# A hybrid decoder layer in split fp32: the sums of the MLP's input, its stores, kept factors of w1 and the late loads change places

## The chip, the cores and the metric

The kernel runs on one core of one Trainium2 chip. A core has five engines with queues of their own: TensorE (PE in the profile; its weight loads are PEld), VectorE (DVE), ScalarE (ACT), GpSimd (POOL) and SyncE (SP), which here only issues DMAs. An engine works through its queue in order. The metric is the device time of one execution in microseconds (us).

## The reference

One decoder layer over 2048 tokens of width 1024, all in fp32:

```python
h = rms_norm(x, mix_norm_pre)
z = h @ w_in                                  # q, k, v, xr, gr
attn = dilated_attention(q, k, v)             # 8 heads, 3 dilations, one joint softmax of the branches
rec  = rg_lru(causal_conv(xr)) * gelu(gr)     # linear recurrence
x = x + rms_norm(concat([attn, rec]) @ w_out, mix_norm_post)
h = rms_norm(x, mlp_norm_pre)
a = relu(h @ w_ff_in)                         # 1024 x 4096
x = x + rms_norm((a * a) @ w_ff_out, mlp_norm_post)
```

## The kernel before

**Products.** A matrix product in fp32 is made of three matmuls in the type fp32r: each operand is split into a high part, a cast by ScalarE, and a low part, operand minus high part (`split`, L52 to L55: the cast is L54, the subtraction L55). The products are high by high, high by low and low by high. Who subtracts is an argument: VectorE as a rule, GpSimd where `lo_eng` says so.

**Stages.** The tokens are worked in two halves of 1024 (`hf` 0 and 1). First come the input projections and the recurrence of both halves, with the attention of half 0. Then, for half 0: the out-projection (`OutProj`; matmuls L778 to L780), the MLP's input (`mlp_in`; L934 to L936) and the MLP's output (`mlp_out`; L1064 to L1066). The attention of half 1 is woven into the MLP's output of half 0 by `interleave`: so many matmul steps of the MLP (`fill`) after each piece of attention. Then come the out-projection and the MLP of half 1. From the out-projection of half 0 on, TensorE's order is the order of the program text. The other engines' order is made by a scheduler that simulates the program; `tc.issue_after(i)` forbids it to issue something ahead of instruction `i`.

**The MLP's input.** `mlp_in` multiplies by a scheme with seven products in place of eight for 2x2 blocks. The right operands B11, B21, B22 and T1 to T4 are sums of blocks of the normed tokens; `Factors.columns` makes B11, B21 and T3 column block by column block while the out-projection runs, `Factors.late` T2, T4, T1 and B22 after it. The left operands come from w1: 16 pairs `j`, each with two loads of 512 KB (`w1r`; for the first two pairs the first of them is `w1f`), four sums on GpSimd (`sub`, L945: S1, S3 in the place of a21, S2, S4 in the place of a12; S1 and S2 are the tiles `ws1` and `ws2`) and seven splits into the tiles `f<half>_<pair>_<product>H` and `L`. A product is 12 matmuls. The program works on two pairs at a time (`TURNS`). ScalarE copies sums out of PSUM (L969 is that of z22 and one of three), VectorE adds, ScalarE squares; `sq` and `as` are what comes out, and SP stores them to DRAM as `sa` (L995, 0.75 MB and L996, 1 MB a pair). `sq`, `as` and `w2s`, the sums of the w2 blocks made on VectorE in half 0 and stored by GpSimd's queue as `sb` (L1007), share a ring of four buffers with one another ("ring r"). A second ring holds six pairs of f tiles, and a third one the w1 tiles.

**The MLP's output.** For each of seven products and 16 `j`, SP loads an `a` and a `b` factor (L1056) from `sa` and from `sb` or `sw2`, and they are split in place (`a_5L` is the low part of a's factor of j 5). At the end of half 1, tokens 12 to 15 get their norm, gain and residual ahead of the last product (`finish`: GpSimd multiplies by the gain, L1097; VectorE adds the residual `x2e`, L1100, loaded at L1095), and tokens 8 to 11 afterwards (`finish_left`, its load is L1109; `finish_right`).

**The join.** At the end of each pair of heads, `join` works out the weights of the branches, stores them (`sco`, L638), loads them back spread over the partitions (`co`, L645), and GpSimd sums the two branches (L647 to L649) and stores them into `smix` (L650). `mix_columns` loads columns of `smix` (L752, 64 KB each, four to a tile `m_0L` or `m_4L`) for the out-projection.

Of the kernel before, what the change touches and what calls it, by code (L numbers as in the profile page):

```python
# [51 lines left out]
def split(nc, hi, lo, src, lo_eng=None):  # L52

    nc.scalar.copy(out=hi, in_=src)  # L54
    return (lo_eng or nc.vector).tensor_tensor(out=lo, in0=src, in1=f32(hi), op=ALU.subtract)  # L55
# [31 lines left out]
class Project:  # L87


    def __init__(self, tc, p, pa, pl, bank, cst, scr, x, xT, g1, w_in):  # L90
# [112 lines left out]
    def qkv(self, hf, pr):  # L203
# [148 lines left out]
def attention(tc, p, bank, cst, scr, hf, mask_a_d, mask_b_d, pj, pw=None, px=None):  # L352
# [255 lines left out]
    def join(pr, st, na, nb):  # L608

        R = 2 * NQH  # L610
        pst = bank("o", f"pst{hf}_{pr}")
# [25 lines left out]
        for i, e in enumerate((eA, eB)):  # L637
            nc.sync.dma_start(out=scr["co"][hf][pr][i].rearrange("h (n j) -> (h n) j", j=P), in_=e)  # L638
        for b in range(NBH):
# [3 lines left out]
            for i in range(2):  # L643
                for u in range(2):
                    nc.sync.dma_start(out=co[i][u * HD:(u + 1) * HD, :],  # L645
                                      in_=scr["co"][hf][pr][i, u:u + 1, cs].partition_broadcast(HD))
# [98 lines left out]
def mix_columns(nc, sh, scr, hf, order, t):  # L745

    mx = {}
    for g0 in range(0, KT, 4):
        n = f"{hf}_{t}_{g0}"
        hi, lo = sh.pair(f"m{n}", (P, 4, P))  # L750
        for i, k in enumerate(order[g0:g0 + 4]):
            nc.sync.dma_start(out=f32(lo[:, i, :]), in_=scr["mix"][hf][k][:, t * P:(t + 1) * P])  # L752
# [154 lines left out]
def mlp_in(tc, sh, scr, hf, H, w1, w2, first):  # L907
# [8 lines left out]
    def pair(j):  # L916
# [4 lines left out]
        def load(f):  # L921
            t = first[j] if f == 0 and j < len(first) else sh.w(f"w1r{n}_{f}", (P, KT, P))
# [22 lines left out]
        sub = lambda o, x, y, op=ALU.subtract: g.tensor_tensor(out=o, in0=x, in1=y, op=op)  # L945
# [10 lines left out]
        S1, S2 = [sh.s(f"ws{i}_{n}", (P, KH, P)) for i in (1, 2)]  # L956
        sub(S1, a21, a22, ALU.add)
        sub(a21, a11, a21)
        factor(7, a21)
        sub(S2, S1, a11)  # L960
        sub(a12, a12, S2)
# [33 lines left out]
        nc.sync.dma_start(out=scr["a"][hf][j][:, 0:3], in_=sq[:, 0:3])  # L995
        nc.sync.dma_start(out=scr["a"][hf][j][:, 3:7], in_=A)  # L996
# [29 lines left out]
TURNS = [(0, 1, 0, 1, 0, 0, 1, 1), (1, 1, 0, 0, 1, 1, 0, 1, 0, 0, 1, 1), (0, 0, 1, 1, 0, 0, 1, 1, 0, 1, 0, 0, 1, 1)]  # L1026


def mlp_out(tc, sh, p, cst, scr, hf, w2, g4, out):
# [52 lines left out]

    def finish(t):
# [10 lines left out]
        x2 = sh.w(f"x2e{tt}")  # L1094
        nc.sync.dma_start(out=x2, in_=scr["x2"][tt])  # L1095
# [8 lines left out]
    def finish_left(t):  # L1104
# [3 lines left out]
        x2 = sh.w(f"x2e{tt}")  # L1108
        nc.sync.dma_start(out=x2, in_=scr["x2"][tt])  # L1109
# [63 lines left out]
def interleave(units, rest):  # L1173
# [20 lines left out]
    for k, (_, turn, values, ending) in enumerate(todo):  # L1194
# [12 lines left out]
        fill(2 - k % 2)  # L1207
# [13 lines left out]
def trunk(tc, x, xT, g1, g2, g3, g4, w_in, conv_w, conv_b, w_r, b_r, w_i, b_i, lam, w_out, w1, w2,  # L1221
# [11 lines left out]
    with (  # L1233
# [16 lines left out]
        def halves(shape, dt, n, nm):  # L1250
# [31 lines left out]
        with contextlib.ExitStack() as st:  # L1282
# [182 lines left out]
```

## Time and profile before

| | |
|---|---|
| median of 3 runs | 2367.01 us (2364.72 to 2367.58) |
| the profiled execution | 2365.82 us |
| its span | 2364.0 us |
| granted TensorE clock, mean | 0.971 |
| busy: TensorE, VectorE, ScalarE, GpSimd | 2200.3, 1526.7, 1236.1, 663.6 us |
| moved by DMA | 451.51 MB |

The profile is of one execution. A row of a group reads: line, engine, operation, output tile <- input tiles, shapes, xcount, then busy time, mean of one in ns, and the time the engine stood idle just before them with what ended it. `<-DVE f_1L L55` reads: until VectorE finished the tile f_1L at line 55. In the table by windows each engine has its busy time in that stretch, followed by the number of its instructions; PEclk is the granted clock, 1.00 being full speed. A row of the waits reads: who waited at which line, for whom, the sum in us, how many times, and the longest.

### The profile page before, as it was taken

Reading aid. Unit: us, or ns where it says so; the run is one execution under the profiler, and the core shown is the slowest. Engines: PE = TensorE matmul, PEld = TensorE weight load, DVE = VectorE, ACT = ScalarE, POOL = GpSimd, SP = SyncE. Lnnn points to the kernel's source line nnn. Section 1 sums busy time; section 2 is a strip of 40 time slices with the busy share of each in tenths; the row PEclk is TensorE's granted clock in tenths of the full one; section 3 lists DMA queues with packets and bytes.
Section 4 is the critical chain, followed back from the end, with each engine's and each line's share of the span. In section 5 each row is a group of like instructions: output and inputs, shape, how many; then the busy total and the mean of one; then the engine's idle time right before and its main releaser. Section 6 shows DMA issues by size and latency. Waiting matters only on the chain.

```text
span 2364.0 us, 31248 instructions
## 1 busy us (share of the span) xinstructions
PE 2200.3 (93%) x10264; PEld 1786.1 (76%) x10264; DVE 1526.7 (65%) x2898; ACT 1236.1 (52%) x2503; POOL 663.6 (28%) x599
## 2 busy tenths in 40 slices
PE   8999999889998999998989998978979999999997
PEld 6678778667886787786877786767868888788885
DVE  6757576885358776774767676856884545545357
ACT  7636464644344554453756567554555555563523
POOL 5543415474525432420001110112353232000012
PEclk9999989899999999999999999999989999999998
DMA  8364674635852467778666686667324434866625
GB/s 282 105 193 148 189 209 146 188 124 158 254 169 94 159 239 288 258 260 297 226 181 214 186 254 189 187 224 213 116 87 145 160 134 163 304 228 196 192 89 191
DMA packets 213523, 451.51 MB, mean 191 GB/s; under 512 B 23040, under 2 KB 77728, under 8 KB 207088
## 3 DMA queue, kind: packets, MB, share of 16 engines
q1 hardware_dynamic: 198160, 386.22, 50.5%
q0 software_dynamic: 15200, 63.29, 8.1%
q8 instruction: 81, 1.33, 0.2%
q14 instruction: 82, 0.67, 0.1%
HBM read 323.46 MB, written 142.74 MB: 197 GB/s over the span
## 4 chain that ended last, share of the span: by engine, by line
PE 63%; DVE 12%; DMA 10%; ACT 4%; issue 4%; POOL 1%; SPq 1%; DVEq 0%; ACTq 0%; POOLq 0%
PE o L1065 7%; PE o L1064 7%; PE o L1066 7%; PE za L934 4%; PE za L936 4%; PE za L935 4%; PE z L198 3%; PE z L200 3%; PE z L199 3%; PE zc L935 2%; PE zc L936 2%; PE zc L934 2%; PE m L780 2%; PE m L778 2%; PE m L779 2%
## 5 line engine op out<-in xcount | busy, mean ns | idle before, releaser
L198 PE MATMUL z<-hH,wH 128*128 128x512 f32 x640 | 263.8, 412 | 14.1 <-ACT wH L54 5.9
L199 PE MATMUL z<-hL,wH 128*128 128x512 f32 x640 | 259.6, 406 | 0.7 <-DVE hL L173 0.7
L200 PE MATMUL z<-hH,wL 128*128 128x512 f32 x640 | 259.2, 406 | 0.0
L198 PEld LDWEIGHTS z<-hH,wH 128*128 128x128 f32 x640 | 122.9, 192 | 47.8 <-ACT wH L54 6.7
L199 PEld LDWEIGHTS z<-hL,wH 128*128 128x128 f32 x640 | 122.8, 192 | 32.5 <-issue 4.8
L200 PEld LDWEIGHTS z<-hH,wL 128*128 128x128 f32 x640 | 122.8, 192 | 28.5 <-issue 3.4
L55 POOL TENSOR_TENSOR wL<-wraw,wH 128x512 fp32r<-128x512 f32 x74 | 106.0, 1447 | 129.4 <-ACT wH L54 123.3
L939 ACT ACTIVATE sq<-sq 128x512 f32<-128x512 f32 x96 | 60.8, 633 | 99.6 <-DVE sq L943 99.6
L413 ACT ACTIVATE smB<-smB,negB 128x128 f32<-128x128 f32 (+3 forms) x128 | 71.5, 559 | 60.4 <-DVE negB L411 60.3
L1097 POOL TENSOR_TENSOR y<-y,g4b 128x512 f32<-128x512 f32 x8 | 11.8, 1506 | 307.1 <-ACT junk_y L84 307.1
L945 POOL TENSOR_TENSOR ws<-w1r 128x512 f32<-128x512 f32 x32 | 47.0, 1469 | 168.2 <-DMA w1r<-in_dram 152.5
L940 ACT ACTIVATE sq<-sq 128x512 f32<-128x512 f32 x128 | 79.1, 629 | 2.0
L936 PE MATMUL za<-hHB,f_1L 128*128 128x512 f32 x128 | 52.4, 409 | 26.2 <-DVE f_1L L55 26.2
L647 POOL TENSOR_TENSOR na<-na,co 128x512 f32<-128x512 f32 x16 | 21.8, 1364 | 195.4 <-DMA co<-sco 195.3
L452 POOL DMA_DIRECT2D va<-sv x32 | 17.5, 556 | 205.6 <-PE oA L531 204.4
L413 ACT ACTIVATE sm<-sm,neg 128x256 f32<-128x256 f32 (+1 forms) x128 | 63.1, 495 | 22.9 <-DVE neg L411 22.5
L54 ACT CAST wH<-wraw 128x512 fp32r<-128x512 f32 (+1 forms) x81 | 47.1, 611 | 53.1 <-PE z L199 34.9
L55 DVE TENSOR_TENSOR tlB<-pT_B,thB 128x384 fp32r<-128x384 f32 x96 | 57.3, 598 | 24.6 <-ACT thB L54 24.0
L1006 DVE TENSOR_TENSOR w2s<-w2s 128x512 f32<-128x512 f32 x64 | 46.2, 722 | 40.0 <-DMA w2s<-in_dram 38.9
L377 PE MATMUL pT_B<-ident,smB 128*128 128x128 f32 x320 | 54.1, 286 | 16.1 <-DVE tlB L55 10.6
L404 DVE CUSTOM_DVE_ANT_0 smB<-SB,mask_b 128x128 f32<-128x128 f32 (+3 forms) x128 | 59.7, 483 | 11.7 <-PE SB L565 7.0
L55 POOL TENSOR_TENSOR zl<-zn,zh 128x512 fp32r<-128x512 f32 x32 | 44.5, 1389 | 77.4 <-ACT zh L54 42.9
(469 smaller groups left out, 7322.0 us busy)
## 6 DMA issues: line engine op xcount, KB each, us to landing
sa<-as SPq DMA_DIRECT2D x32, 1024.0 KB, 5.0
w1r<-in_dram SPq DMA_DIRECT2D x60, 512.0 KB, 4.2
sa<-sq SPq DMA_DIRECT2D x32, 768.0 KB, 3.3
wraw<-in_dram SPq DMA_DIRECT2D x79, 256.0 KB, 3.8
w2s<-in_dram SPq DMA_DIRECT2D x16, 1024.0 KB, 7.9
sb<-w2s POOLq DMA_DIRECT2D x16, 1024.0 KB, 7.2
kh<-sk SPq DMA_DIRECT2D x24, 512.0 KB, 6.1
kl<-sk SPq DMA_DIRECT2D x24, 512.0 KB, 6.7
```

Of the source, the lines that this page charges most:

```text
L55: return (lo_eng or nc.vector).tensor_tensor(out=lo, in0=src, in1=f32(hi), op=ALU.subtract)
L198: pe.matmul(z, hi[:, k, :], hh, start=(k == 0), stop=False)
L199: pe.matmul(z, hi[:, k, :], hl, start=False, stop=False)
L200: pe.matmul(z, lo[:, k, :], hh, start=False, stop=(k == KT - 1))
L413: s.activation(out=sm[:, c0:c0 + w], in_=sm[:, c0:c0 + w], func=AF.Exp, bias=neg[:, j:j + 1], accum_out=st[:, 1, u, cols[j]:cols[j] + 1])
L934: pe.matmul(o, hi[:, k], bh[:, k], start=start and k == 0, stop=False, skip_group_check=True)
L935: pe.matmul(o, hi[:, k], bl[:, k], start=False, stop=False, skip_group_check=True)
L936: pe.matmul(o, lo[:, k], bh[:, k], start=False, stop=k == KH - 1, skip_group_check=True)
L940: s.activation(out=z, in_=z, func=AF.Square)
L1064: pe.matmul(o, ah[:, ts], bh, start=fresh and j == 0, stop=False, skip_group_check=True)
L1065: pe.matmul(o, ah[:, ts], bl, start=False, stop=False, skip_group_check=True)
L1066: pe.matmul(o, al[:, ts], bh, start=False, stop=j == NJ - 1, skip_group_check=True)
```

## The change

Eight edits are made at once.

1. **Sums on VectorE.** The four sums of a pair in `mlp_in` go from GpSimd to VectorE: 128 instructions on GpSimd before (4 for each of 16 pairs in two halves), 120 on VectorE after (8 go with edit 4). In `Factors`, the sums of B11 and B21 for column blocks 2 and 3 of the second half of the tokens (`sums`) and all of T1 are VectorE's; column blocks 0 and 1 stay on GpSimd. The order of the late operands is fixed by a list of steps: a step of pair 0 or 1 alternates with T2, T4, T1 and B22, and each may not be issued ahead of what the one before it made.
2. **Stores.** `sa` is stored by GpSimd's queue and no longer by SP's.
3. **Join.** In half 1, `sco` and `co` go through GpSimd's queue and no longer through SP's.
4. **Kept factors.** Half 0 stores 16 split factors of w1 (all seven of pairs 0 and 1, the first two of pair 2; high and low, 256 KB each, 32 DMAs on GpSimd's queue) in DRAM as `sf`. Half 1 loads them on SP, 32 DMAs, instead of splitting them again; pairs 0 and 1 there need no w1 load, no sum and no split.
5. **x2.** The loads of `x2e` at the end of half 1 may not be issued ahead of the last load of an `a` or `b` factor.
6. **Mix.** `smix` is one tensor for each half, and four loads of 64 KB are one load of 256 KB. The first of half 1 come after the last factor load of half 0's MLP output; those of half 0 come earlier.
7. **First phase.** The recurrence products r10 to r13 come after the pool of half 0's attention is closed; the splits of the projections q11 to q13 have their low part on VectorE.
8. **Weave.** `FIRSTFILL` is 32 for 36, and the last pieces of attention are followed by one step where there were two or one, so that seven more steps of the MLP's output are left after the attention. (A step is the three matmuls of one token block.)

TensorE has 9559 rows in both programs, VectorE 2764 before and 2887 after, ScalarE 2056 and 2026, GpSimd 563 and 507, SP 1113 and 972.

```diff
         def load(f):
-            t = first[j] if f == 0 and j < len(first) else sh.w(f"w1r{n}_{f}", (P, KT, P))
+            if hf and j < 2:
+                return None, None
+            t = place[j] if f == 0 and j < 2 else sh.w(f"w1r{n}_{f}", (P, KT, P))
...
         def factor(m, src):
             f[m] = sh.pair(f"f{n}_{m}", (P, KH, P))
-            split(nc, *f[m], src)
+            kept = [(scr["f"][j, m][i], f32(t).rearrange("p k t -> p (k t)")) for i, t in enumerate(f[m])] if m in AHEAD.get(j, ()) else []
+            if hf and kept:
+                for d, t in kept:
+                    nc.sync.dma_start(out=t, in_=d)
+                return
+            sh.made = split(nc, *f[m], src)
+            for d, t in kept:
+                g.dma_start(out=d, in_=t)
...
-        sub = lambda o, x, y, op=ALU.subtract: g.tensor_tensor(out=o, in0=x, in1=y, op=op)
+        sub = lambda o, x, y, op=ALU.subtract: v.tensor_tensor(out=o, in0=x, in1=y, op=op)
...
-        nc.sync.dma_start(out=scr["a"][hf][j][:, 0:3], in_=sq[:, 0:3])
-        nc.sync.dma_start(out=scr["a"][hf][j][:, 3:7], in_=A)
+        g.dma_start(out=scr["a"][hf][j][:, 0:3], in_=sq[:, 0:3])
+        g.dma_start(out=scr["a"][hf][j][:, 3:7], in_=A)
```

```diff
-            self.split("T3", t3, cs)
-            e = v if c == TB // P - 1 else g
-            e.tensor_tensor(out=b11[:, :, cs], in0=t3[:, :, cs], in1=b11[:, :, cs], op=ALU.add)
-            e.tensor_tensor(out=b21[:, :, cs], in0=b21[:, :, cs], in1=b11[:, :, cs], op=ALU.subtract)
+            self.done = self.split("T3", t3, cs)
+            if c < 2:
+                self.sums(g, cs)
...
+            if b == "T2" and c > 1:
+                self.sums(v, cs)
+            if b == "T1":
+                v.tensor_tensor(out=t2[:, :, cs], in0=b22[:, :, cs], in1=t2[:, :, cs], op=ALU.subtract)
...
-                        for j in (2, 0, 1):
-                            next(pairs[j])
-                        with tc.issue_after(op.scaled.ins), tc.issue_after(op.rooted.ins):
-                            F.late(F.LATE, range(4))
+                    for j in (2, 0):
+                        next(pairs[j])
+                    made = F.done
+                    for step in (1, "T2", 0, "T4", 1, "T1", 0, 1, "B22"):
+                        with tc.issue_after(made[0].ins), tc.issue_after(made[1].ins):
+                            if step in F.LATE:
+                                made = F.late(step)
+                            else:
+                                next(pairs[step])
+                                made = made if hf else sh.made
```

```diff
+        dma = (g if hf else nc.sync).dma_start
...
-            nc.sync.dma_start(out=scr["co"][hf][pr][i].rearrange("h (n j) -> (h n) j", j=P), in_=e)
+            dma(out=scr["co"][hf][pr][i].rearrange("h (n j) -> (h n) j", j=P), in_=e)
...
-                    nc.sync.dma_start(out=co[i][u * HD:(u + 1) * HD, :],
-                                      in_=scr["co"][hf][pr][i, u:u + 1, cs].partition_broadcast(HD))
+                    dma(out=co[i][u * HD:(u + 1) * HD, :],
+                        in_=scr["co"][hf][pr][i, u:u + 1, cs].partition_broadcast(HD))
...
-        for i, k in enumerate(order[g0:g0 + 4]):
-            nc.sync.dma_start(out=f32(lo[:, i, :]), in_=scr["mix"][hf][k][:, t * P:(t + 1) * P])
+        k0 = order[g0]
+        nc.sync.dma_start(out=f32(lo), in_=scr["mix"][hf][k0:k0 + 4, :, t * P:(t + 1) * P].rearrange("k p t -> p k t"))
...
-                ready = [mix_columns(nc, sh, scr, 1, order, t) for t in range(2)]
                 run_all(rest)
+                with tc.issue_after(cst["load"].ins):
+                    ready = [mix_columns(nc, sh, scr, 1, order, t) for t in range(2)]
...
+    def load_x2(tt):
+        x2 = sh.w(f"x2e{tt}")
+        with tc.issue_after(cst["load"].ins):
+            nc.sync.dma_start(out=x2, in_=scr["x2"][tt])
+        return x2
...
-        fill(2 - k % 2)
+        fill(1 if k + n >= len(todo) else 2 - k % 2)
...
-FIRSTFILL = 36
+FIRSTFILL = 32
...
-ORDER = "q00 r02 q01 a0 r03 q02 a1 q03 x2 x3 a2 q10 a3 r10 r11 r12 r13 q11 q12"
-LATER = "q13"
+ORDER = "q00 r02 q01 a0 r03 q02 a1 q03 x2 x3 a2 q10 a3"
+BETWEEN = "r10 r11 r12 r13"
+LATER = "q11 q12 q13"
```

VectorE where the MLP's input of half 0 begins, before: `f0_2_1L` is the low part that pair 2's first product waits for, `hLT3` belongs to T3, `hLT2`, `hLT4`, `hLT1` and `hLB22` to the late operands, `h2r` and `x2_7`, `xt7` to the normed tokens.

```order
L55 TENSOR_TENSOR hLT3_0_6276<-h2r0_12_6267,hHT3_0_6275 128x4x128
...
L815 SCALAR_TENSOR_TENSOR xt7_7032<-x2_7_7128,nm_x7_7127,g3b0_0_6288 128x512
...
L55 TENSOR_TENSOR hLT2_0_7159<-h2r0_11_6269,hHT2_0_7158 128x4x128 x2
L55 TENSOR_TENSOR hLT4_0_7161<-h2r0_21_6268,hHT4_0_7160 128x4x128 x2
L55 TENSOR_TENSOR hLB22_0_7165<-h2r0_22_6270,hHB22_0_7164 128x4x128 x3
L55 TENSOR_TENSOR f0_2_1L_7259<-w1r0_2_0_7256,f0_2_1H_7258 128x512
L55 TENSOR_TENSOR f0_2_2L_7292<-w1r0_2_0_7256,f0_2_2H_7291 128x512
...
L55 TENSOR_TENSOR f0_0_7L_7315<-w1r0_0_1_7217,f0_0_7H_7314 128x512
...
L55 TENSOR_TENSOR hLT1_0_7163<-h2r0_11_6269,hHT1_0_7162 128x4x128 x2
...
L888 TENSOR_TENSOR h2r0_11_6269<-h2r0_12_6267,h2r0_11_6269 128x4x128
L55 TENSOR_TENSOR hLT3_0_6276<-h2r0_12_6267,hHT3_0_6275 128x4x128
```

After, the same place; `ws`, `w1r` and `place` are the four sums of a pair:

```order
L808 TENSOR_TENSOR x2_7_7082<-x2_7_7082,xt7_6986 128x512
L882 TENSOR_TENSOR h2r0_12_6289<-h2r0_22_6292,h2t0_6_0_7146 128x4x128
L966 TENSOR_TENSOR w1r0_0_1_7173<-place0_0_6302,w1r0_0_1_7173 128x512
...
L966 TENSOR_TENSOR ws2_0_0_7273<-ws1_0_0_7272,place0_0_6302 128x512
...
L55 TENSOR_TENSOR hLT3_0_6298<-h2r0_12_6289,hHT3_0_6297 128x4x128
L55 TENSOR_TENSOR f0_2_1L_7219<-w1r0_2_0_7216,f0_2_1H_7218 128x512
L966 TENSOR_TENSOR place0_0_6302<-place0_0_6302,ws2_0_0_7273 128x512
...
L55 TENSOR_TENSOR f0_2_2L_7252<-w1r0_2_0_7216,f0_2_2H_7251 128x512
L55 TENSOR_TENSOR f0_0_7L_7277<-w1r0_0_1_7173,f0_0_7H_7276 128x512
...
L816 SCALAR_TENSOR_TENSOR xt7_6986<-x2_7_7082,nm_x7_7081,g3b0_0_6310 128x512
```

`f0_2_1L` stood behind seven splits of the late operands; now it stands behind the T3 split of column block 2 and ahead of all of the late ones, and the four sums of pair 0 stand around it.

SP at the end of the attention of half 1, before: `sco` and `co` are the join's, `woL` the weights of the next out-projection, `a0_4_14L` and its like the factors of the MLP's output, `m1_` the columns for the out-projection.

```order
L638 DMA sco1_3_102<-jt1_3_14566 16x128 x2
...
L645 DMA co1_3_0_14581<-sco1_3_102 64x512 x4
L645 DMA co1_3_1_14590<-sco1_3_102 64x512 x4
...
L1056 DMA a0_4_13L_14809<-sa0_13_148 128x512
...
L752 DMA m1_0_0L_14836<-smix1_4_115 128x128
...
L752 DMA m1_0_4L_14844<-smix1_2_113 128x128
L786 DMA xt8_14998<-in_0_dram 128x1024
...
L752 DMA m1_0_4L_14844<-smix1_3_114 128x128
L752 DMA m1_1_0L_14852<-smix1_4_115 128x128
...
L752 DMA m1_1_4L_14860<-smix1_3_114 128x128
L1056 DMA a0_4_14L_14868<-sa0_14_149 128x512
...
L1056 DMA b0_4_15L_14895<-sb15_182 128x512
```

After:

```order
L1081 DMA a0_4_12L_14773<-sa0_12_133 128x512
...
L1081 DMA a0_4_13L_14800<-sa0_13_134 128x512
...
L1081 DMA a0_4_14L_14822<-sa0_14_135 128x512
L1081 DMA b0_4_14L_14827<-sb14_167 128x512
L1081 DMA a0_4_15L_14844<-sa0_15_136 128x512
L1081 DMA b0_4_15L_14849<-sb15_168 128x512
L753 DMA m1_0_0L_14934<-smix1_104 128x4x128
L753 DMA m1_0_4L_14939<-smix1_104 128x4x128
L753 DMA m1_1_0L_14944<-smix1_104 128x4x128
L753 DMA m1_1_4L_14949<-smix1_104 128x4x128
```

The join's rows are gone from this queue, and the factors of j 14 and 15 stand ahead of the columns, where they stood behind 16 column loads.

SP at the last product of half 1, before: `x2e` is the residual, `b1_3_` the last product's factors.

```order
L1095 DMA x2e12_20588<-sx212_131 128x1024
...
L1095 DMA x2e14_20632<-sx214_133 128x1024
L1095 DMA x2e15_20654<-sx215_134 128x1024
L1109 DMA x2e8_20673<-sx28_127 128x1024
...
L1056 DMA b1_3_3L_20460<-sw23_186 128x512
...
L1056 DMA b1_3_4L_20470<-sw24_187 128x512
...
L1109 DMA x2e9_20681<-sx29_128 128x1024
...
L1109 DMA x2e10_20689<-sx210_129 128x1024
...
L1109 DMA x2e11_20697<-sx211_130 128x1024
...
L1056 DMA b1_3_15L_20580<-sw215_198 128x512
```

After:

```order
L1081 DMA b1_3_3L_20378<-sw23_172 128x512
...
L1081 DMA b1_3_4L_20388<-sw24_173 128x512
...
L1081 DMA b1_3_15L_20498<-sw215_184 128x512
L1111 DMA x2e12_20506<-sx212_117 128x1024
L1111 DMA x2e13_20528<-sx213_118 128x1024
...
L1111 DMA x2e15_20572<-sx215_120 128x1024
L1111 DMA x2e8_20591<-sx28_113 128x1024
...
L1111 DMA x2e9_20599<-sx29_114 128x1024
...
L1111 DMA x2e11_20615<-sx211_116 128x1024
```

All eight `x2e` loads stand behind the last factor load, where five stood ahead of the last product's loads and three among them.

More of the change, by code (lines that the diff above doesn't have):

```diff
@@ L52, in split @@
 def split(nc, hi, lo, src, lo_eng=None):
[L54 to L55 removed]
+    return (nc.scalar.copy(out=hi, in_=src),
+            (lo_eng or nc.vector).tensor_tensor(out=lo, in0=src, in1=f32(hi), op=ALU.subtract))
 def rsqrt_mean(nc, pool, ss, k, name, eps, e=None):
@@ L955, in pair @@
         yield
[L956 to L961, printed above, removed]
+        if hf and j < 2:
+            S1 = S2 = None
+            factor(7, None)
+        else:
+            S1, S2 = [sh.s(f"ws{i}_{n}", (P, KH, P)) for i in (1, 2)]
+            sub(S1, a21, a22, ALU.add)
+            sub(a21, a11, a21)
+            factor(7, a21)
+            sub(S2, S1, a11)
+            sub(a12, a12, S2)
         c = sh.bank("B", f"zc{n}")
@@ L1093, in finish @@
             return
-        x2 = sh.w(f"x2e{tt}")
-        nc.sync.dma_start(out=x2, in_=scr["x2"][tt])
+        x2 = load_x2(tt)
         for ds in (left, right):
@@ L1257, in trunk @@
             "co": halves([2, 2, HT], F32, NP, "co"),
-            "mix": halves([P, HT], F32, KT, "mix"),
+            "mix": [d.tile([KT, P, HT], F32, name=f"smix{hf}") for hf in range(2)],
             "x2": [d.tile([P, D], F32, name=f"sx2{i}") for i in range(S // P)],
@@ L1301, in trunk @@
                 pj.load_norm(3, px)
-            products = [(t[0], *map(int, t[1:])) for t in f"{ORDER} {LATER}".split() if t[0] in "qr"]
+            products = [(t[0], *map(int, t[1:])) for t in f"{ORDER} {BETWEEN} {LATER}".split() if t[0] in "qr"]
             copies = [(scr["wout"][k], w_out[k]) for k in order]
@@ L1334, in trunk, with half @@
                 run(ORDER)
+            pg = per.enter_context(sb("g2", "right"))
+            sh = Shared(pg, bank)
+            run(BETWEEN)
             lst.close()
-            pg = per.enter_context(sb("g2", "right"))
             wo = load_wo(0)
+            pj.lo = nc.vector
             run(LATER)
-        sh = Shared(per.enter_context(sb("px", "left")), pg, bank)
-        def half(hf, wo, ready=None):
+            ready = [mix_columns(nc, sh, scr, 0, order, t) for t in range(2)]
+        sh.px = per.enter_context(sb("px", "left"))
+        def half(hf, wo, mx):
             with contextlib.ExitStack() as st:
@@ L1346, in half @@
                 h2 = {}
-                with sb(f"op{hf}", "left") as po:
-                    first = [po.tile([P, KT, P], F32, tag="w1f", bufs=2, name=f"w1f{hf}_{j}") for j in range(2)]
+                po = st.enter_context(sb(f"op{hf}", "left"))
+                with contextlib.nullcontext():
+                    place = [po.tile([P, 4, TB], F32, name="place1")] if hf else [
+                        po.tile([P, KT, P], F32, name=f"place0_{j}") for j in range(2)]
                     op = OutProj(tc, sh, po, scr, hf, wo, order, x, g2, g3)
@@ L1385, in trunk @@
         with per, tc.manual_schedule(engines={mybir.EngineType.PE}):
-            end = half(0, wo)
+            end = half(0, wo, ready)
             with sb("y0", "left") as p:
```

56 lines of the change are left out of this document (29 added, 27 removed).

## The prediction

> **What bounds the kernel now.** First the page: engines and the chain that ended last.
>
> ```profile
> PE 2200.3 (93%) x10264; PEld 1786.1 (76%) x10264; DVE 1526.7 (65%) x2898; ACT 1236.1 (52%) x2503; POOL 663.6 (28%) x599
> PE 63%; DVE 12%; DMA 10%; ACT 4%; issue 4%; POOL 1%; SPq 1%; DVEq 0%; ACTq 0%; POOLq 0%
> ```
>
> TensorE is busy 93% and both programs give it the same 9559 rows, so the change can only win what TensorE loses: 163.7 us without work, and more at a lowered clock. The windows by stage say where.
>
> ```profile
> 0.00:580.00 580.00, 531.72 (x2576) 423.09 (x2577) 406.11 (x850) 326.59 (x675) 265.41 (x269) 0.96 0.57 175
> 744.00:775.00 31.00, 17.91 (x80) 14.26 (x79) 30.51 (x33) 11.71 (x25) 21.34 (x15) 0.78 0.21 68
> 775.00:1075.00 300.00, 291.78 (x1252) 235.85 (x1251) 212.35 (x283) 156.32 (x280) 100.30 (x80) 0.99 0.68 245
> 1075.00:1125.00 50.00, 39.95 (x160) 31.43 (x159) 22.68 (x42) 19.04 (x31) 0.55 (x1) 0.90 0.96 319
> 1125.00:1575.00 450.00, 417.97 (x2260) 347.16 (x2259) 316.65 (x766) 282.81 (x631) 46.03 (x56) 0.98 0.67 203
> 1575.00:1603.00 28.00, 13.94 (x43) 9.94 (x43) 9.28 (x14) 10.45 (x18) 13.56 (x12) 0.76 0.74 248
> 1705.00:1745.00 40.00, 26.91 (x113) 21.55 (x112) 38.79 (x47) 17.21 (x34) 25.33 (x16) 0.79 0.20 66
> 1745.00:2020.00 275.00, 274.98 (x1198) 224.15 (x1197) 144.21 (x202) 150.96 (x263) 78.92 (x56) 1.00 0.42 152
> 2020.00:2060.00 40.00, 36.66 (x152) 29.05 (x151) 27.13 (x42) 25.75 (x44) 0.00 (x0) 0.96 0.86 311
> 2060.00:2300.00 240.00, 240.00 (x1059) 198.52 (x1058) 108.79 (x177) 99.53 (x183) 1.64 (x2) 1.00 0.59 187
> 2300.00:2364.00 64.00, 46.81 (x186) 34.92 (x184) 47.45 (x90) 25.42 (x55) 16.82 (x11) 0.89 0.49 177
> ```
>
> The columns are PE, PEld, DVE, ACT, POOL (busy us, number), granted clock, DMA share, GB/s. Two rows never wait: 275/1198 = 0.230 us a matmul in the MLP's input and 240/1059 = 0.227 in its output. With these, lost time (clock included) is 300 - 1252 x 0.230 = 12 us in the input of half 0; 50 - 160 x 0.227 = 13.7 where its output begins; 28 - 43 x 0.227 = 18.2 at the end of the attention of half 1; 40 - 152 x 0.227 = 5.5 where the output of half 1 begins. Which waits these are:
>
> ```profile
> PE za L936 <- DVE f_1L L55: 26.2, 2, 13.1
> PE o L1065 <- DVE b_3L L55: 9.1, 2, 8.9
> PE za L934 <- ACT sq L969: 8.0, 3, 4.2
> PE o L1064 <- ACT b_12H L54: 7.6, 1, 7.6
> PE o L1064 <- ACT b_14H L54: 6.1, 1, 6.1
> PE o L1064 <- ACT b_2H L54: 6.1, 2, 4.1
> PE o L1064 <- ACT b_3H L54: 5.8, 2, 4.9
> ```
>
> Two waits of 13.1 us stand where the MLP's input of each half begins. After the first, TensorE is slow too:
>
> ```profile
> 769.96 0.80 PE L936 MATMUL za<-hHB,f_1L 128*128 128x512 f32 x1 [13.09 <-DVE f_1L L55]
> ...
> 773.84 0.38 PE L876 MATMUL h2t<-ident,xt 128*128 128x128 f32 x2
> ```
>
> Ten matmuls lie between these rows, 3.9 us for 2.3: each such wait costs 13.1 + 1.6 = 14.7 us. Why VectorE is late shows in its own rows and GpSimd's:
>
> ```profile
> 750.47 5.18 DVE L55 TENSOR_TENSOR hLT<-h2r,hHT 128x512 fp32r<-128x512 f32 x1
> ...
> 756.22 1.41 DVE L815 SCALAR_TENSOR_TENSOR xt<-x,nm_x,g3b 128x512 f32<-128x512 f32 x2
> 757.55 6.75 DVE L55 TENSOR_TENSOR hLT<-h2r,hHT 128x512 fp32r<-128x512 f32 x4
> 764.22 5.08 DVE L55 TENSOR_TENSOR hLB<-h2r,hHB 128x512 fp32r<-128x512 f32 x3
> 769.23 0.68 DVE L55 TENSOR_TENSOR f_1L<-w1r,f_1H 128x512 fp32r<-128x512 f32 x1
> 769.83 0.68 DVE L55 TENSOR_TENSOR f_2L<-w1r,f_2H 128x512 fp32r<-128x512 f32 x1
> ```
>
> ```profile
> 753.80 1.29 POOL L945 TENSOR_TENSOR ws<-ws,w1f 128x512 f32<-128x512 f32 x1
> 757.05 1.70 POOL L945 TENSOR_TENSOR ws<-w1r 128x512 f32<-128x512 f32 x1 [1.95 <-DVE xt L815]
> ```
>
> VectorE takes 0.60 us an operation alone and 1.7 beside GpSimd's (6.75/4), one even 5.18; and seven late splits that nobody waits for yet, 11.8 us, stand ahead of f_1L. The Trainium skill, SBUF — State Buffer, "SBUF: two separate sides", says that a VectorE operation with two SBUF inputs and a GpSimd one that reads SBUF shut each other out for a whole instruction; these rows agree.
>
> **The change part by part.** The sum is made from 2365.8 us, the profiled execution; the median is 1.2 higher.
>
> *A, input of half 0 begins.* In the new order f0_2_1L stands right behind the T3 split of column block 2. That split's 5.18 us become 0.6, three sums add 1.8: f0_2_1L ends near 753, ahead of TensorE's need at 769.96 - 13.09 = 756.9. All 14.7 go. What is late next: VectorE now does all the sums. The last block's normed tokens, xt, are there at 757.6; eight transposes between TensorE's products, a copy, a subtraction, a cast and a low part bring its T3 split to about 762 (an estimate from such operations of 0.6 us each). From there T2 needs 13 operations, 13 x 0.6 = 8, and is ready at 770; TensorE has four products of 12 x 0.23 = 2.7 us from 756.9 and asks at 767.8: about 2.5 lost. T1 needs 18 more, 11 us, to 781, while two products last to 775.5: 5.5 lost. Gain 14.7 - 8 = +7, between 0 (the chain slips by another 7, if casts on ScalarE don't keep pace) and 14.
>
> *B, input of half 1 begins.* The same wait, and there pairs 0 and 1 need no sum and no split: 14 splits and 8 sums, 22 x 0.6 = 13 us less on VectorE than in A, which covers A's 8. Their 32 loads of 256 KB, 8 MB at the 245 GB/s of the input of half 0, take 34 us, begun during the out-projection. +13, between 5 (loads wait for the ring of six) and 14.7.
>
> *C, rest of the input of half 0.* VectorE gets 4 x 0.6 = 2.4 us a pair, 34 us for 14 pairs, on 212 of 300; GpSimd's sums go and with them the 1.7 us doubles. The lost 12 us come from ring r, whose buffers wait for stores to land:
>
> ```profile
> ACT sq L969 <- DMA sa<-as: 22.8, 10, 5.9
> sa<-as SPq DMA_DIRECT2D x32, 1024.0 KB, 5.0
> sb<-w2s POOLq DMA_DIRECT2D x16, 1024.0 KB, 7.2
> ```
>
> A store of 1 MB takes 5.0 us from SP and 7.2 from GpSimd's queue, +2.2; against this, it no longer queues behind w1 loads on SP. I take 0, between -15 (half of 2.2 x 14 passed on) and +8 (the 8.0 of the third wait row goes).
>
> *D, output of half 0 begins.* SP no longer holds sa0_14 and sa0_15 ahead of b_3L. But the DMA share is 0.96 there. The Trainium skill, Trainium Kernel Development and Optimization, "Key Constraints", says that DMAs from all queues share the same 16 engines and another queue only saves issue time; by it D would be 0 and the sum below 4 smaller. I take +4 for the order alone (a third of 13.7), between 0 and 8.
>
> *E, end of the attention of half 1.*
>
> ```profile
> 1571.56 4.93 SPq L645 DMA_DIRECT2D co<-sco  x8
> ...
> 1580.81 3.26 SPq L752 DMA_DIRECT2D m_0L<-smix  x4
> ...
> 1594.28 0.36 SPq L1056 DMA_DIRECT2D a_14L<-sa  x1
> ```
>
> The two waits (7.6 and 6.1) come from b_12L behind the co loads, and from a_14L behind 16 column loads. Both orders go. What an issue costs on GpSimd's queue, a group of such issues shows:
>
> ```profile
> L452 POOL DMA_DIRECT2D va<-sv x32 | 17.5, 556 | 205.6 <-PE oA L531 204.4
> ```
>
> Ten issues of 0.56 us for sco and co, and two landings up to 2.2 us later as in C, let the join's chain end 4 to 8 us later; seven more steps, 7 x 3 x 0.227 = 4.8 us, cover part. Of 18.2 I take +9, between -2 and 14.
>
> *F, output of half 1 begins.* Stores leave SP: of 5.5, +3 (0 to 4).
>
> *G, the end.*
>
> ```profile
> 2308.86 5.16 DVE L1100 SCALAR_TENSOR_TENSOR y<-y,r_y,x2e 128x512 f32<-128x512 f32 x3
> 2313.94 1.75 DVE L55 TENSOR_TENSOR b_3L<-b_3L,b_3H 128x512 fp32r<-128x512 f32 x1
> ```
>
> ```profile
> 2356.80 0.39 PE L1066 MATMUL o<-b_15H,a_15L 128*128 128x512 f32 x1
> ```
>
> b_3L waits behind three residuals, which now come after the last factor: 5.1 of the 8.9 go. TensorE ends at 2357.2 having lost 57.2 - 186 x 0.227 = 15 since 2300; the rest is loads behind x2e on SP, and clock. +7 (3 to 11). The 8 residuals, 5.5 us, and their loads go beside the last half product's 21 us and cost nothing; if that cover is gone, 3.
>
> *H.* The first phase and the attention get another order and GpSimd's share of the woven joins: -3 (-9 to +5).
>
> Sum: 7 + 13 + 0 + 4 + 9 + 3 + 7 - 3 = 40. 2365.8 - 40 = 2325.8, as a median 2327.
>
> **The rivals.** 0.2% (4.7 us) is about what a measurement of this kernel can tell from no change.
>
> *VectorE binds the start of half 0* (A = 0) and stores lengthen ring r (C = -8): 2327 + 15 = 2342. For it: VectorE is busy 30.51 of 31.00 there. Against: most of that is doubles that go.
>
> *The join is late* (E = -2, with 4 more in H): 2342. For it: software-queue landings as in C.
>
> *Kept factors arrive late* in half 1 (B = 0): 2340. Against: a DMA share of 0.20 there.
>
> *Slower: ring r holds every pair of half 0.* GpSimd's queue is in order: a sb store that waits for VectorE's w2 sums holds the sa stores behind it, and VectorE is now busier. If each of 14 pairs pays the largest wait of ring r, 4.2, that is 59: 2327 + 59 = 2386. It decides from 40/14 = 2.9 us a pair. Against: half of ScalarE's waits on sa pass unseen (22.8 there, 8.0 on TensorE). The Trainium skill, SBUF — State Buffer, "SBUF: two separate sides", has a rule this way: VectorE operations of some kinds keep GpSimd from writing the descriptors of its DMAs. 7.2 against 5.0 agrees in sign; no run here shows the cause.
>
> *The gains cancel* (A, D, E 0, C -15, H -5): 40 - 7 - 4 - 9 - 15 - 2 = 3 left: 2364, no change. That the change doesn't do what it says is excluded for the order, which the rows show, not for the times.
>
> **How the numbers follow.** Forecast 0.52, first rival 0.18, join 0.10, kept factors 0.08, ring 0.06, cancelled 0.06. Faster 0.88, same 0.06, slower 0.06. The range: the terms' half widths (7, 5, 11.5, 4, 8, 2, 4, 7) make 19 together by squares; so 2308 below, and above it takes in the three rivals at 2340 to 2342 with some of their spread: 2349.
>
> **What would show it.** Right: no wait for f_1L over 3 us; waits for hLT or hLB splits of T2 and T1 of 2 to 6 us instead in half 0 and none in half 1; no waits for b_12H, b_14H; b_3L under 5 us. Wrong: sq waits for sa of over 3 us a pair on TensorE; m_4L late by over 5 us; f loads as a releaser of za; sa landings over 10 us.

## The result and the profile after

The changed kernel takes 2355.26 us (2354.24 to 2361.97, 7 runs) where the kernel before takes 2367.58 us beside it: a ratio of 0.9947 (0.9929 to 0.9966). It is faster by 0.5%, 12 us; 40 were forecast, and the range ended 6 us lower. The profiled execution spans 2353.5 us, against 2364.0.

The page's engines and chain after:

```profile
PE 2201.1 (94%) x10264; PEld 1789.5 (76%) x10264; DVE 1532.4 (65%) x3042; ACT 1228.7 (52%) x2487; POOL 489.7 (21%) x567
PE 57%; DMA 13%; DVE 10%; issue 9%; ACT 4%; POOL 2%; SPq 1%; DVEq 0%; POOLq 0%; ACTq 0%
```

GpSimd has 174 us less work, VectorE 6 more, and DMA's share of the chain rose from 10% to 13%. The windows are cut where TensorE's stages change, so that a row stands against the same work of before. After:

```profile
1077.00:1118.00 41.00, 25.37 (x99) 19.84 (x99) 13.93 (x23) 11.14 (x19) 6.61 (x12) 0.79 0.98 321
1118.00:1574.00 456.00, 408.17 (x2194) 340.37 (x2192) 301.65 (x749) 275.46 (x613) 61.88 (x86) 0.96 0.65 192
1574.00:1617.00 43.00, 35.42 (x154) 27.33 (x151) 27.90 (x47) 22.68 (x41) 17.84 (x21) 0.92 0.90 299
1715.00:1755.00 40.00, 37.67 (x168) 29.74 (x168) 29.29 (x55) 20.34 (x41) 1.58 (x2) 1.00 0.67 219
```

Before, the stage of the second row, cut the same way:

```profile
1122.00:1558.00 436.00, 404.95 (x2196) 337.10 (x2195) 305.23 (x749) 275.22 (x615) 46.03 (x56) 0.98 0.66 202
```

The attention of half 1 does the same work on TensorE (2194 and 2196 records), VectorE (749 both) and ScalarE, and takes 456 us where it took 436. The input of half 1 (last row of after) begins with hardly a wait. The waits of TensorE after:

```profile
PE o L1089 <- ACT b_3H L54: 15.3, 1, 15.3
PE pT_B L377 <- DVE tlB L55: 13.8, 5, 6.3
PE za L955 <- ACT sq L994: 10.2, 4, 4.4
PE pT_B L377 <- DVE na L398: 10.0, 2, 6.0
PE o L1089 <- ACT b_11H L54: 7.1, 1, 7.1
PE za L956 <- DVE hLT L55: 5.1, 3, 2.0
PE o L1090 <- DVE b_3L L55: 2.8, 1, 2.8
```

Both 13.1 us waits for f_1L are gone. New are 10.0 us for `na` in the attention (1.7 before) and one of 15.3 for b_3H where the output of half 0 begins.

For a balance of all stages, each interval between the starts of two matmuls is set against the tenth percentile of its kind (same output tile, same shapes), and the excess is summed: "lost" holds waits and lowered clock alike. In us, from one profile each, which need not be of a median execution (those of e3 and e12 are the longest of their runs, those of e4 and e6 the shortest); e1 and e12 are experiments below.

| stage | before | after | e1: join on SP | e12: e1, stores of half 0 on SP |
|---|---|---|---|---|
| first phase | 147.9 | 146.0 | 146.8 | 148.0 |
| out-projection 0 and 1 | 13.9 | 14.9 | 12.9 | 12.5 |
| input of half 0, first 330 matmuls | 18.2 | 17.5 | 17.7 | 13.0 |
| input of half 0, rest | 14.5 | 12.0 | 12.1 | 14.1 |
| output of half 0 begins | 15.1 | 18.8 | 17.9 | 14.6 |
| attention of half 1 | 91.5 | 113.2 | 96.8 | 99.6 |
| after the attention | 20.3 | 11.1 | 9.2 | 8.2 |
| input of half 1, first 330 | 18.7 | 5.6 | 5.7 | 5.6 |
| output of half 1 begins | 6.2 | 5.8 | 5.2 | 6.5 |
| end | 15.4 | 6.5 | 6.5 | 6.4 |
| sum, with the stages that lose 3.6 in each | 365.4 | 355.0 | 334.4 | 332.2 |

The difference of the sums, 10.4 us, is that of the spans, 10.5.

What the attention waits for, at the second join. Some names first: `qs` are the queries of the next head (512 KB) and `qa` VectorE's copy of them, a cast; `smB` are a head's scores, `negB` the negated maximum of a row, which ScalarE's exponential needs; `na` is a sum that VectorE makes at the end of a block of attention. After, on SP, GpSimd, VectorE and ScalarE in turn:

```profile
1353.42 2.62 SPq L428 DMA_DIRECT2D qs<-sq  x1
1356.18 0.57 SPq L1081 DMA_DIRECT2D a_13L<-sa  x1
```

```profile
1353.21 4.12 POOL L646 DMA_DIRECT2D co<-sco  x8 [1.12 <-DMA sco<-jt]
```

```profile
1359.33 0.08 DVE L404 DVE_READ_ACCUMULATOR2_ANT stB<- 128x1 f32 x1
1366.59 1.06 DVE L430 CAST qa<-qs 128x512 fp32r<-128x512 f32 x2 [7.18 <-DMA qs<-sq]
1367.57 0.14 DVE L411 TENSOR_SCALAR negB<-stB 128x1 f32<-128x1 f32 x1
```

```profile
1367.74 0.72 ACT L413 ACTIVATE smB<-smB,negB 128x512 f32<-128x512 f32 x1 [9.54 <-DVE negB L411]
```

Before, on SP and on VectorE:

```profile
1352.12 5.03 SPq L645 DMA_DIRECT2D co<-sco  x8
1357.19 0.60 SPq L428 DMA_DIRECT2D qs<-sq  x1
```

```profile
1359.65 0.15 DVE L411 TENSOR_SCALAR negB<-stB 128x1 f32<-128x1 f32 x1
1361.51 1.97 DVE L430 CAST qa<-qs 128x512 fp32r<-128x512 f32 x2 [1.71 <-DMA qs<-sq]
1363.40 0.67 DVE L398 TENSOR_TENSOR na<-oA,fold 64x512 f32<-64x512 f32 x1
```

Counted from the first issue of `co`, `qs` is issued 0.2 us later where it was 5.1, and yet is there after 13.4 us where it was 9.4: it was in flight together with the eight `co` loads and the next factors. Before, `co` went first through the same queue, and `qs` followed when most of `co` had landed. The DMA share, the last column but one, is 0.99 in that stretch after and 0.75 before:

```profile
1353.00:1367.00 14.00, 10.94 (x59) 9.03 (x57) 4.96 (x12) 4.24 (x11) 7.92 (x11) 0.97 0.99 266
```

```profile
1352.00:1362.00 10.00, 10.00 (x61) 8.77 (x60) 6.36 (x15) 5.87 (x14) 5.71 (x5) 1.00 0.75 225
```

A second thing changed with the queue: the order that the scheduler makes. After, the cast of `qs` stands in VectorE's queue ahead of `negB`, and ScalarE's exponential waits for that; before, `negB` stood ahead of the cast. TensorE's wait is for `na`, which stands behind the cast in both. So VectorE waits longer for `qs`, and more stands behind that wait. Both hold at the first join too, and no run separates the two cleanly.

### The profile page after: what moved, and what is told of

The parts are those of the page before. It is cut to its first block, busy times and chain, and to the rows that moved or that the text cites. A ratio compares the mean times of both kernels' runs of the same rounds, so it can differ in the third digit from the quotient of the medians.

```text
span 2353.5 us, 31020 instructions
## 1 busy us (share of the span) xinstructions
PE 2201.1 (94%) x10264; PEld 1789.5 (76%) x10264; DVE 1532.4 (65%) x3042; ACT 1228.7 (52%) x2487; POOL 489.7 (21%) x567
## 4 chain that ended last, share of the span: by engine, by line
PE 57%; DMA 13%; DVE 10%; issue 9%; ACT 4%; POOL 2%; SPq 1%; DVEq 0%; POOLq 0%; ACTq 0%
PE o L1090 6%; PE o L1089 6%; PE o L1091 6%; PE za L955 4%; PE za L956 4%; PE za L957 4%; PE z L198 2%; PE z L200 2%; PE z L199 2%; PE zc L956 2%; PE zc L955 2%; PE zc L957 2%; PE m L781 2%; PE m L780 2%; PE m L779 2%
## 5 line engine op out<-in xcount | busy, mean ns | idle before, releaser
L198 PE MATMUL z<-hH,wH 128*128 128x512 f32 x640 | 264.5, 413 | 13.4 <-ACT wH L54 6.1
L55 POOL TENSOR_TENSOR wL<-wraw,wH 128x512 fp32r<-128x512 f32 x58 | 84.6, 1471 | 114.0 <-ACT wH L54 107.9
L1020 POOL DMA_DIRECT2D sa<-sq x31 | 16.6, 534 | 400.9 <-ACT sq L961 400.2
L377 PEld LDWEIGHTS pT_B<-ident,smB 128*128 128x128 f32 x320 | 38.1, 147 | 46.5 <-DVE tlB L55 16.1
L955 PE MATMUL za<-hHT,f_6H 128*128 128x512 f32 x128 | 53.2, 416 | 10.2 <-ACT sq L994 10.2
L1099 DVE TENSOR_TENSOR y<-o,y 128x512 f32<-128x512 f32 x24 | 16.2, 683 | 69.7 <-PE o L1091 69.7
L54 ACT CAST thB<-pT_B 128x384 fp32r<-128x384 f32 x96 | 48.6, 508 | 20.3 <-PE oB L590 14.1
```

The lines of the kernel that those rows point to most:

```text
L54: return (nc.scalar.copy(out=hi, in_=src), (lo_eng or nc.vector).tensor_tensor(out=lo, in0=src, in1=f32(hi), op=ALU.subtract))
L198: pe.matmul(z, hi[:, k, :], hh, start=(k == 0), stop=False)
L955: pe.matmul(o, hi[:, k], bh[:, k], start=start and k == 0, stop=False, skip_group_check=True)
```

## The experiments

Theory J: the join on GpSimd's queue costs the attention its 20 us, as those rows show it. Rival W: the weave does, with fewer steps of the MLP beside the attention. Rival S: the stores on GpSimd's queue.

**e1: join on SP.**

```diff
-        dma = (g if hf else nc.sync).dma_start
+        dma = nc.sync.dma_start
```

> The changed kernel with the join of half 1 (sco and co) back on SP's queue, all else as changed. Theory J (the 18 us that the attention of half 1 lost come from co landing after 7.7 us instead of 3.2 beside the next heads' loads): TensorE's loss from 1125 to 1575 us falls from 111 us to 93 to 100, the three waits of 4 to 6 us behind the qs cast go, and the kernel takes 2355 - 15 = about 2340 us, less what the end of the attention gives back (7 us). Theory W (the 18 us come from the weave, four steps fewer ahead of the attention and seven fewer in it): the loss there stays at 105 to 115 us and the time rises by the 7 us at the end, about 2362 us.

Measured: 2332.57 us (2321.66 to 2337.22), ratio 0.9843 (0.9806 to 0.9880), 23 us under the changed kernel. The attention takes 440 us, the table has 96.8 for 113.2, and the waits for `na` sum to 3.9:

```profile
1118.00:1558.00 440.00, 405.07 (x2196) 338.28 (x2194) 306.56 (x749) 275.01 (x613) 45.75 (x56) 0.97 0.66 199
```

Theory J holds. Of the 21.7 us that the attention lost, 16.4 come back; with `sco` and `co` both on SP, the seven runs of the changed kernel lie between 93.5 and 99.6, against 91.5 before, and what holds the rest isn't known. The end of the attention gave nothing back (9.2 for 11.1), against the expectation. `negB` stands ahead of the cast at the first two joins again, as before.

**e2: weave as before.**

```diff
-            fill(1 if k + n >= len(todo) else 2 - k % 2)
+            fill(2 - k % 2)
...
-FIRSTFILL = 32
+FIRSTFILL = 36
```

> The changed kernel with the weave as before (36 steps ahead of the attention, two or one after each of the last pieces). Theory W: the loss from 1125 to 1575 us falls to 93 to 100 us, the 15.3 us wait for b_3H where the output of half 0 begins falls to 5 to 10, and the kernel takes about 2340 us. Theory J: the loss of the attention stays at 105 to 115 us, and the end of the attention loses 5 us more for want of steps: about 2358 us.

Measured: 2354.06 us (2333.02 to 2362.39), ratio 0.9933 (0.9904 to 0.9961); attention 119.4 lost, and the wait for b_3H still 15.3. Rival W falls; the ten executions spread wider than those of any other run.

**e3: all sa stores on SP.** Edit: `g.dma_start` becomes `nc.sync.dma_start` in the two stores.

> The changed kernel with the sa stores back on SP's queue. If the stores on GpSimd's queue cost the 4 us of the rest of half 0's input and the 6 us where its output begins: 2345 us, and the wait for b_3H falls from 15.3 to about 5 to 10. If they gain, as forecast for the order of SP's queue, or if the 15.3 us wait comes from the attention's loads alone: 2355 to 2362 us, the 15.3 staying.

Measured: 2353.21 us (2351.20 to 2364.22), ratio 0.9940 (0.9917 to 0.9963). The output of half 0 begins with 15.2 for 18.8 lost (two waits of 4 us for 15.3), that of half 1 loses 10.2 for 5.8, and the attention 119.2. Rival S falls as the cause of the 20 us; by these profiles the stores' queue gives and takes some 4 us a place.

**e4: join, weave and stores as before.**

> The changed kernel with all three (join, weave, stores) as before; what stays is sums on VectorE, kept factors, late x2 and mix loads, and the first phase's order. If the gains that were met (7 at the input of half 0, 12 at that of half 1, 9 at the end, 8 at the end of the attention) need none of the three: 2367 - 7 - 12 - 9 - 4 = 2335 us, with the attention's loss at 90 to 98 us. If the attention's loss comes from the order of VectorE and ScalarE that the scheduler makes and not from queues or weave, it stays at 105 to 115 us and the time is about 2352 us.

Measured: 2333.43 us (2328.64 to 2334.55), ratio 0.9849 (0.9822 to 0.9877), attention 94.1 lost. What stays of the change makes a gain of 34 us without any of the three.

**e9: the kernel before, with the join on GpSimd's queue alone.** Edit: `join`'s lines of the change's diff, in the kernel before.

> The kernel before with one part of the change alone: in half 1, sco and co on GpSimd's queue. Theory J1 (co's eight loads on a queue of their own run beside qs, a and b loads on the same DMA engines, and VectorE and ScalarE stand in order behind the casts of those loads): the loss in the attention rises from 91 us to 105 to 112, co's last landing comes 11 to 14 us after its first issue instead of 6 to 8, and the kernel takes 10 to 20 us more than before, 2377 to 2387 us. Theory J2 (the move only costs together with the other edits, by the order the scheduler then makes): within 4 us of before.

Measured: 2387.81 us (2386.55 to 2396.01), ratio 1.0090 (1.0069 to 1.0110): 20.5 us slower. The attention loses 116.6 for 91.5, and three waits are longer than before (6.1, 10.6 and 1.7 there; the first lies behind the attention):

```profile
PE o L1065 <- ACT b_14H L54: 13.9, 1, 13.9
PE pT_B L377 <- DVE tlB L55: 12.0, 5, 4.5
PE pT_B L377 <- DVE na L398: 11.8, 2, 8.4
```

The last landing of `co` comes 12 to 15 us after its first issue at the first three joins, as expected; before it was 8 at the first and already 13 at the third. J1 holds, J2 falls as worded, since the move costs without the other edits. But here too the cast of `qs` has come ahead of `negB` at the first two joins, so the scheduler's order is part of what the move does.

**e5 and e6: which half of the join.** e5 has `co` on SP and `sco` on GpSimd's queue, e6 the reverse.

> The changed kernel with co back on SP and sco left on GpSimd's queue. J1 (the loads of co do the harm): about 2333 us as with both on SP, attention's loss 94 to 99 us. If the two stores of sco, landing after 4.5 us, do it by making the join late: 2345 to 2355 us.

> The changed kernel with sco back on SP and co left on GpSimd's queue. J1: 2350 to 2356 us, attention's loss 108 to 115 us. If sco does the harm: about 2335 us.

Measured: e5 2341.40 us (2337.36 to 2345.22), ratio 0.9888 (0.9868 to 0.9909), attention 105.6; e6 2349.88 us (2344.36 to 2355.97), ratio 0.9923 (0.9901 to 0.9944), attention 109.1. e6 is as expected, e5 isn't: `sco` costs some 9 us by itself, though the interval of e5 still touches that of e1. In e5, SP can issue `co` only when `sco` has landed, and `qs` stands behind: at the first join `sco` is there after 5.6 us, and SP issues `co` 0.02 us later. At the second `sco` takes 1.6 us, but the eight issues take long:

```profile
1355.96 8.41 SPq L646 DMA_DIRECT2D co<-sco  x8
1364.41 0.60 SPq L428 DMA_DIRECT2D qs<-sq  x1
```

In e1 the same eight issues take 4.97 us and `qs` follows at 1356.74. `co` alone costs more: 12 us in the attention and 17 in the time (e6 against e1). The waits for `na` follow the same order in all runs: 1.2 to 4.1 us where both are on SP, 5.8 in e5, 8.3 in e6, and 10.0 to 17.7 where both are on GpSimd's queue.

**e7: e1 without kept factors.** Edit: `AHEAD = {}`, and the branches for pairs 0 and 1 of half 1 taken out; pair 1's `sq` there is in ring r again.

> The changed kernel with the join on SP and without kept factors: half 1 loads w1, sums and splits for pairs 0 to 2 as half 0 does, nothing is stored for it. If the forecast's working for the input of half 1 holds (the kept factors cover the 8 us that VectorE's sums cost at the start of an input), the loss at the start of half 1's input rises from 5.7 to 12 to 15 us and the time from 2333 to 2341 us. If the order of the steps alone took the 13.1 us wait away: 2333 to 2335 us.

Measured: 2332.97 us (2330.52 to 2338.06), ratio 0.9854 (0.9837 to 0.9870): as e1. Half 1's input does lose 12.2 instead of 5.7, but half 0's first part loses 11.8 instead of 17.7. The kept factors save 6.5 us and cost 5.9.

**e8: e1, the pairs' sums of half 0 on GpSimd.** Edit: `(v if hf else g)` in `sub`.

> The changed kernel with the join on SP and the four sums of a pair back on GpSimd in half 0 alone. If the sums on VectorE are what takes the first 13.1 us wait away (GpSimd's operations lengthened VectorE's from 0.6 to 1.7 us): the loss in the first part of half 0's input rises from 17.7 by 5 to 10 us, a wait for a low part of f or hL of over 3 us comes back, and the time is 2338 to 2343 us. If the fixed order of the steps is enough: 2331 to 2335 us, and the rest of that input, with 34 us less on VectorE, loses no more than 12.

Measured: 2339.33 us (2334.63 to 2349.37), ratio 0.9895 (0.9865 to 0.9925). The first part loses 20.3 for 17.7, the rest 15.8 for 12.1, with waits for hLT up to 5.0 and for sq up to 7.9. The time and the wait of 5.0 are as the first reading had them, but the wait of 13.1 does not come back: the pairs' sums on VectorE did not take it away. What is left is the fixed order of the steps, with the `Factors` sums that stayed on VectorE here; no run moves those alone. The pairs' sums are worth some 6 us on top by the balance, and the intervals of e8 and e1 overlap.

**e10: e1, x2 loads early. e11: e1, column loads ahead.** Edits: each takes one `issue_after(cst["load"].ins)` away, and e11 puts the columns ahead of `run_all(rest)`.

> The changed kernel with the join on SP and the x2e loads free to be issued ahead of the last factor loads, as before. If the forecast's working for the end holds: the loss at the end rises from 6.5 to 12 to 16 us with the wait for b_3L back at 8 to 9, and the time from 2333 to 2339 to 2342 us. If the end gains from something else: 2333 us.

> The changed kernel with the join on SP and the first column loads of half 1's out-projection ahead of the last factor loads in the program, free of the wait for them, as before. If the place of the column loads is what gained at the end of the attention: the loss after the attention rises from 9 to 14 to 18 us (a wait for b_14 of some 6 us comes back) and the time to 2338 to 2342 us. If one load of 256 KB for four of 64 KB, or the seven more steps, gained it: 2331 to 2335 us.

Measured: e10 2340.27 us (2337.75 to 2344.57), ratio 0.9895 (0.9860 to 0.9930), the end loses 15.4 for 6.5; e11 2343.73 us (2338.23 to 2346.97), ratio 0.9905 (0.9869 to 0.9942), 26.8 for 9.2 after the attention. The intervals of both still touch that of e1, but waits like those of before are back, first in e10, then in e11:

```profile
PE o L1090 <- DVE b_3L L55: 8.9, 1, 8.9
```

```profile
PE o L1089 <- ACT b_13H L54: 7.6, 1, 7.6
PE o L1089 <- ACT b_14H L54: 4.3, 1, 4.3
```

**e12: e1, stores of half 0 on SP.** Edit: `(g if hf else nc.sync)` in the two stores.

> The changed kernel with the join on SP and the sa stores of half 0 on SP, those of half 1 left on GpSimd's queue. If the 32 stores of kept factors hold the first sa stores behind them on GpSimd's queue: the loss in the first part of half 0's input falls from 17.7 to about 12, the start of the output of half 0 from 18 to 15, and the time to 2325 to 2329 us. If the stores' queue makes no difference: 2331 to 2335 us.

Measured: 2324.17 us (2322.86 to 2332.15), ratio 0.9832 (0.9795 to 0.9869), the lowest median of all, 43 us under the kernel before; its interval overlaps e1's, so the step from e1 isn't shown by the times. The first part of half 0's input loses 13.0 for 17.7, the start of its output 14.6 for 17.9. The first stores of the changed kernel, on GpSimd's queue, and what ScalarE waited for them:

```profile
785.26 0.54 POOL L949 DMA_DIRECT2D sf<-f_3L  x1 [1.82 <-DVE f_3L L55]
787.07 0.54 POOL L949 DMA_DIRECT2D sf<-f_4L  x1
796.19 0.54 POOL L1020 DMA_DIRECT2D sa<-sq  x1 [8.58 <-ACT sq L961]
800.27 0.55 POOL L1021 DMA_DIRECT2D sa<-as  x1 [3.53 <-DVE f_6L L55]
```

```profile
ACT sq L994 <- DMA sa<-as: 12.8, 6, 5.5
```

By the trace the last `sf` has landed at 793.2, so the kept factors don't stand ahead of the `sa` stores on the way, as expected here. The 1 MB store issued at 800.3 lands 8.3 us later, and sq waits 5.5 for it; the same store takes 5.3 us in e12 and 5.1 in e7, and TensorE's waits for sq in this part fall from 4.8 us to 1.0 in both. By which way the `sf` stores lead to the slower landing stays open.

## Why the prediction was wrong

**H is the step that failed:** "The first phase and the attention get another order and GpSimd's share of the woven joins: -3 (-9 to +5)". The first phase gained 1.9 and the attention lost 21.7, so that this term misses by 17 of the 30 us between the forecast of 40 and the 10.4 of the balance; D misses by 8, A by 6, F by 3, and C and G give 4 back. I had priced the join's move at its own end alone (E, after the last of four joins) and by its result being late. It acts in each of the first three joins: in the 50 us around them (from 5 us ahead of the first `co`) the changed kernel loses 12.4, 13.9 and 20.4 us, e1 8.5, 7.8 and 14.2. At the first two it acts by the loads that fly beside `co`, behind whose casts VectorE and ScalarE stand in order, and by the earlier place of the cast of `qs`. The before trace bore the hint: `co` landed after 3.1 us on SP, where loads behind it were held back for the 5 us of its eight issues.

The third join is another case, and its cause is not settled. There `co` lands after 3.0 us, with nothing issued beside it on SP, and VectorE does not wait for `qs`. TensorE's longest wait there that e1 has not is this one:

```profile
1489.68 1.08 PE L377 MATMUL pT_B<-ident,smB 128*128 128x128 f32 x4 [4.96 <-ACT b_5H L54]
```

```profile
1483.66 5.15 DVE L55 TENSOR_TENSOR b_4L<-b_4L,b_4H 128x512 fp32r<-128x512 f32 x1 [0.35 <-ACT b_4H L54]
...
1488.86 0.68 DVE L398 TENSOR_TENSOR na<-oA,fold 64x512 f32<-64x512 f32 x1
```

```profile
1482.96 1.63 POOL L648 TENSOR_TENSOR na<-na,co 128x512 f32<-128x512 f32 x1
...
1486.68 1.57 POOL L649 TENSOR_TENSOR nb<-nb,co 128x512 f32<-128x512 f32 x1
```

VectorE's subtraction takes 5.15 us beside four of GpSimd's sums, where its like takes 0.7, and `na`, which ends at 1489.5, stands behind it. ScalarE's cast of the late factor b_5, which TensorE's row names, ends at 1489.6. Which of the two held TensorE isn't shown. e6 has the same long subtraction (5.32 us); e1 has two such operations too (4.27 and 5.14 us) but loses less there.

**A, +7:** the 13.1 us wait went, and T2 and T1 of half 0 wait 3.5 of the 5.1 in the hLT row (8 forecast), but 4.8 us of new waits for sq came and the first part gained only 0.7; 5.2 with the stores of half 0 on SP (e12). **B, +13:** 13.1 measured; the working was right for half 1 and left out what the 32 stores cost half 0 (e7). **C, 0:** +2.5. **D, +4:** -3.7. The order of SP's queue changed as shown, but b_3H came 15.3 us late at a DMA share of 0.98. With the stores of half 0 back on SP the stage loses 15.2 (e3) and 14.6 (e12), as before (15.1), so the stores' queue is what cost it. The rule of the Trainium skill cited there (Trainium Kernel Development and Optimization, "Key Constraints"), that DMAs from all queues share the same 16 engines, spoke for 0 and was the better guide. **E, +9:** 9.2, by the place of the column loads: with them early again the stage loses 26.8 (e11), more than the 20.3 before. The forecast had it from both orders together, and one wait like the old ones stayed (b_11H, 7.1). **F, +3:** 0.4. **G, +7:** 8.9, by the x2 loads (e10).

Without the join's move the total comes near: e1 is 36 us under the kernel before where 40 were forecast, and e12 43. That is in part luck, since A and D fell short there as well (0.5 and -2.8 in e1).

Of the signs named for being right most came: no long wait for f_1L, waits for T2 and T1 of 3.5 us, b_3L at 2.8. They spoke for the terms that were worked out. None of them looked at the attention, where the forecast failed.

**The rivals.** The late join had the right edit, with the wrong place and a smaller price: 15 us against the forecast, where e9 has 20.5 and e1 23. Ring r did not hold the pairs: ScalarE's waits for sa fell from 22.8 us to 12.8. The rule of the Trainium skill named there (SBUF — State Buffer, "SBUF: two separate sides"), that some VectorE operations keep GpSimd from writing descriptors, was not tested. `sa` on GpSimd's queue landed after 6.2 us at the median, against 5.0 on SP before; but in e12, the lowest median, half 0's took 9.0 on SP.

## What to carry to other kernels

When a transfer moves to a second queue, price every transfer that used to stand behind it, not only its own lateness: here SP's queue had held `qs` back until most of `co` was there. Ask then which engine has a cast of such a load at the head of its queue, with urgent work behind, and look whether the scheduler has moved that cast. And take a change of eight edits apart at once: one of these eight took back 24 of 36 us (e1), and costs 20.5 alone (e9).

## What the runs showed that was not expected

The same eight loads of 128 KB land after 3.0 us on SP's queue and 7.7 on GpSimd's (e1 and the changed kernel, medians in the attention):

```profile
co<-sco SPq DMA_DIRECT2D x29, 128.0 KB, 3.0
```

```profile
co<-sco POOLq DMA_DIRECT2D x24, 128.0 KB, 7.7
```

Taken join by join, it is not the queue that decides. The changed kernel's medians at the first, second and third join, all on GpSimd's queue:

```profile
co<-sco POOLq DMA_DIRECT2D x8, 128.0 KB, 8.1
co<-sco POOLq DMA_DIRECT2D x8, 128.0 KB, 8.9
co<-sco POOLq DMA_DIRECT2D x8, 128.0 KB, 3.0
```

On SP's queue, the kernel before has 3.1, 3.2 and, at its third join, this:

```profile
co<-sco SPq DMA_DIRECT2D x8, 128.0 KB, 9.0
```

In these four stretches the landing goes with how full the DMA engines are. Their share is 0.99 at the second join of the changed kernel and 0.53 at the third; before, it is 0.75 at the second and 1.06, as the profile counts it, at the third:

```profile
1475.00:1482.00 7.00, 6.45 (x28) 5.27 (x27) 5.07 (x14) 6.92 (x13) 5.09 (x9) 0.72 0.53 176
```

```profile
1466.00:1479.00 13.00, 10.19 (x44) 7.87 (x44) 10.66 (x24) 10.78 (x20) 5.08 (x6) 0.87 1.06 292
```

So GpSimd's way of feeding its queue does not by itself make `co` late: at the third join it feeds the same loads, and they land as fast as on SP. What the move did at the first two is to let loads fly together that one queue had kept apart. The whole stage moved about as much (192 and 199 GB/s).
